# Attention probabilities turned by a VectorE block transpose and transfers inside SBUF, in place of identity products on TensorE

## The chip, the core and the metric

The kernel runs on one core of a Trainium2 chip. The metric is the device time of one execution in microseconds (us). The engines are named as the profile names them: PE is the matrix engine (PEld its weight loads), DVE the vector engine, ACT the scalar engine, POOL the GpSimd engine, and SP the engine whose queue issues nearly all DMA transfers here. SBUF is the on-chip memory of 128 partitions, PSUM the accumulators that PE writes.

## The reference, cut to what matters

Two layers over 256 tokens of width 1024, all in float32. Each layer has a token mixer and a gated MLP with a residual sum each:

```python
xn = rmsnorm(h) * norm1
u, q, k, v, g_pool, g_attn = split(xn @ w_in)        # widths 1024, 1536, 1536, 1536, 1024, 1024
pooled = centred_mean(u, windows 2/4/8/16) - u ;  pool_out = (pooled @ w_pool) * pool_scale
for g, (window, dilation) in enumerate(((128, 1), (512, 4), (2048, 16))):   # 4 heads of 128 each
    logits = q_g @ k_g.T * 128**-0.5 + rel_bias[bucket(j - i)][:, heads of g]    # keys out of reach: -1e30
    o_g, lse_g = softmax(logits) @ v_g, logsumexp(logits)
attn = sum_g softmax_over_groups(lse)_g * o_g
merged = sigmoid(g_pool) * (pool_out @ w_a) + sigmoid(g_attn) * (attn @ w_b)
h = h + merged @ w_o
h = h + (gelu(conv3(rmsnorm(h) @ w_up_a)) * (rmsnorm(h) @ w_up_g)) @ w_down
```

The three groups share one normalisation: the weighting by the groups' softmax denominators equals one softmax over all the keys of the three groups together. The kernel uses that.

## The kernel before, in words

**Precision by parts.** A product of two float32 matrices is made from fp32r parts: each operand is split into a high part (an ACT cast) and a low part (a DVE subtraction of the cast from the original), and high x high, low x high and high x low are summed in PSUM. Every weight goes through this split on the chip: class `Weights` loads 1 MB pieces on SP's queue into three buffers `raw` (line 117), casts them on ACT (line 177, `wh`) and subtracts on DVE (line 178, `wl`). Five pairs of `wh`/`wl` exist, and the split runs three pieces ahead of the product that uses it. The dilated groups 1 and 2 of attention stay in plain f32.

**Tokens.** Tokens are stored by parity: row m of tile t holds token 2m + t. So the 256 tokens are two tiles of 128 rows; the 256 keys of group 0, and for groups 1 and 2 the 128 keys of the same parity, make 512 columns of scores for each head and tile.

**One layer.** Values are made first, then the eight columns of the pooling branch (`proj`, lines 482 and 484 for its two runs of products), then queries and keys in six rounds of `PAIRS` with four projections each. From round 3 on attention is interleaved: after some of the projections one step is taken from a list, `steps`; the rest of the list is used up during the eight projections by `w_a`. For the heads of a layer the steps are

- `scores(hh)`: for each tile t, products of queries and keys into one PSUM tile `s_ps` (lines 870 and 875), DVE adds the bias from the table `bt` (881) and finds the row maximum (886), ACT takes the exponential and the row sum (889), DVE divides by the sum (891, 892);
- `turn(hh)`: the probabilities have queries on the partitions, and the product with the values needs keys there. Per tile four 128x128 blocks are turned by products with an identity matrix (904) into PSUM `pt_ps`; ACT and DVE copy them out as a high part `pth` (905) and low part `ptl` (910) for group 0, and in f32 as `pt` for groups 1 and 2 (907, 909);
- `weigh(hh)`: products of values and turned probabilities into `o_ps` (921, 925), split into `at2`.

The list takes the heads in pairs (a, b): scores a, turn a, scores b, weigh a, turn b, weigh b.

**The bias table.** `load_bias` loads the bias rows `rel_bias` (32 buckets by 12 heads) and a one-hot table of 33 rows by 5 kinds of 256 offsets. `build_bias` makes one product per kind from 33 rows with the high and one with the low part of the bias (line 374, `f_ps`), interleaved with the first projections of the pooling branch in layer 0. The result goes through DRAM (`fd`, then `sk` with 128 copies), and five loads with a skewed row pitch fetch it as `bt`.

**What sets the order.** The code is written as one stream. A scheduler turns it into one fixed order for each engine and for SP's queue, and inserts the semaphore waits; buffers of one tag are reused in turn (`bufs` says how many). An engine works off its order strictly, so whatever waits holds up what stands behind it. DMA completions are counted on eight semaphores used in turn, so a DMA also waits for the one issued eight before it.

Of the kernel before, what the change touches and what calls it, by code (L numbers as in the profile page):

```python
# [10 lines left out]
F32 = mybir.dt.float32  # L11
F32R = mybir.dt.float32r
# [4 lines left out]
P = 128  # L17
# [5 lines left out]
HPG = 4  # L23
NG = 3
NH = HPG * NG
# [8 lines left out]
NT = 5  # L34
# [5 lines left out]
ENTRY = 4  # L40
# [164 lines left out]
def encoder(ctx, tc, x, w_in, w_pool, pool_scale, w_a, w_b, w_o, norm1, norm2, w_up, conv_w,  # L205
            conv_b, w_down, rel_bias, norm_f, onehot, edges, out):
    nc = tc.nc
    const = ctx.enter_context(tc.tile_pool(name="const", bufs=1))
    wpool = ctx.enter_context(tc.tile_pool(name="weights", bufs=1))
    big = ctx.enter_context(tc.tile_pool(name="big", bufs=1))  # L210
    sm = ctx.enter_context(tc.tile_pool(name="small", bufs=2))
    acc = ctx.enter_context(tc.tile_pool(name="acc", bufs=4, space=bass.MemoryType.PSUM))
# [139 lines left out]
    bt = const.tile([P, HPG, NT * P], F32, name="bt")  # L352

    def load_bias():
        oh = big.tile([33, NT * 256], F32, tag="ybig", name="onehot_sb")
        nc.sync.dma_start(out=oh, in_=onehot)
        rb = sm.tile([33, NH], F32, tag="rb", bufs=1, name="rb")
        nc.vector.memset(rb, 1.0)
        nc.sync.dma_start(out=rb[0:32, :], in_=rel_bias)
        rh = sm.tile([33, NH], F32R, tag="ms", name="rh")  # L360
        rl = sm.tile([33, NH], F32R, tag="ms", name="rl")
        nc.vector.tensor_copy(rh, rb)
        nc.vector.tensor_sub(out=rl, in0=rb, in1=rh.bitcast(F32))
        ohr = big.tile([33, NT * 256], F32R, tag="m2", name="onehot_r")
        nc.scalar.copy(out=ohr, in_=oh)
        return rh, rl, ohr

    def build_bias(rh, rl, ohr):

        fsb = big.tile([HPG, NT * 256], F32, tag="q1", name="fsb")  # L370
        for n, g in enumerate((0, 0, 0, 1, 2)):
            ps = acc.tile([P, 512], F32, tag="acc", name="f_ps")
            for j, r in enumerate((rh, rl)):
                nc.tensor.matmul(
                    ps[:HPG, :256], r[:, g * HPG : (g + 1) * HPG], ohr[:, n * 256 : (n + 1) * 256],
                    start=(j == 0), stop=(j == 1),
                )
            nc.vector.tensor_copy(fsb[:, n * 256 : (n + 1) * 256], ps[:HPG, :256])
            yield

        n = HPG * NT * 256
        fd = dram.tile([1, n], F32, name="fd")
        nc.sync.dma_start(out=fd[0].rearrange("(h e) -> h e", h=HPG), in_=fsb)
# [190 lines left out]
    def v_sum(ps, x2, t, n, piece):  # L574
# [3 lines left out]
        for m, (part, w, j) in enumerate(passes):  # L578
# [2 lines left out]
                stop=(n == 3 and m == 5),  # L581
            )

    def two_parts(tag, name):


        return big.tile([P, KD, 2, 2, P], F32R, tag=tag, name=name)

    def begin_values_of_x():
# [24 lines left out]

        def square(t, n):
            cc = HALVES[n]
            junk = sm.tile([P, 512], F32, tag="p", bufs=3, name="junk")
            if n == 0:
                nc.scalar.activation(
                    junk, h[:, t, cc], AF.Square, scale=D**-0.5, accum_out=ss[t][:, n : n + 1]  # L620
                )
            else:
                nc.vector.scalar_tensor_tensor(
                    out=junk, in0=h[:, t, cc], scalar=1.0 / D, in1=h[:, t, cc],
                    op0=ALU.mult, op1=ALU.mult, accum_out=ss[t][:, n : n + 1],
                )
            if n == 0:
                nc.gpsimd.tensor_scalar_add(ss[t][:, 3:4], ss[t][:, 0:1], EPS)
            else:
                nc.gpsimd.tensor_add(out=ss[t][:, 3:4], in0=ss[t][:, 3:4], in1=ss[t][:, 1:2])  # L630
                return nc.gpsimd.tensor_tensor(out=rs[t], in0=ss[t][:, 3:4], in1=mhalf, op=ALU.pow)
# [117 lines left out]
    for l in range(DEPTH):  # L749
# [43 lines left out]
        g2 = gain(norm2[l])  # L793


        plh = big.tile([P, KD, 2, P], F32R, tag="ybig", name="plh")
# [67 lines left out]
        probs, ptiles = {}, {}  # L864

        def scores(hh):
            for t in range(2):
                ps = acc.tile([P, 512], F32, tag="acc", name="s_ps")
                for m, (a, b) in enumerate(((qh, kh), (qh, kl), (ql, kh))):
                    nc.tensor.matmul(  # L870
                        ps[:, 0:256], a[:, hh, t, :], b[:, hh].rearrange("p t m -> p (t m)"),
                        start=(m == 0), stop=(m == 2),
                    )
# [6 lines left out]
                s = sm.tile([P, 512], F32, tag="s", name="s")  # L880
                nc.vector.tensor_add(
                    out=s.rearrange("p (a b) -> p a b", a=2), in0=ps.rearrange("p (a b) -> p a b", a=2),
                    in1=bias_of(t, hh),
                )
                nm = sm.tile([P, 1], F32, tag="nm", name="nm")
                nc.vector.tensor_reduce(out=nm, in_=s, axis=AX.X, op=ALU.max, negate=True)
                z = sm.tile([P, 1], F32, tag="z", name="z")
                p = sm.tile([P, 512], F32, tag="p", bufs=3, name="p")
                nc.scalar.activation(p, s, AF.Exp, bias=nm[:, 0:1], accum_out=z)
                rz = sm.tile([P, 1], F32, tag="rz", name="rz")  # L890
                nc.vector.reciprocal(rz, z)
                nc.vector.tensor_scalar(
                    out=p, in0=p, scalar1=rz[:, 0:1], scalar2=0.5, op0=ALU.mult, op1=ALU.mult
                )
                probs[hh, t] = p

        def turn(hh):
            pth = sm.tile([P, 2, 2, P], F32R, tag="pth", bufs=1, name="pth")
            ptl = sm.tile([P, 2, 2, P], F32R, tag="us", name="ptl")
            pt = sm.tile([P, 2, 2, P], F32, tag="pt", bufs=1, name="pt")  # L900
            for t in range(2):
                ps = acc.tile([P, 4, P], F32, tag="acc", name="pt_ps")
                for b in range(4):
                    nc.tensor.transpose(ps[:, b, :], probs[hh, t][:, b * P : (b + 1) * P], ident)  # L904
                nc.scalar.copy(out=pth[:, :, t, :], in_=ps[:, 0:2, :])
                if t == 0:
                    nc.scalar.copy(out=pt[:, :, t, :], in_=ps[:, 2:4, :])
                else:
                    nc.vector.tensor_copy(pt[:, :, t, :], ps[:, 2:4, :])
                nc.vector.tensor_sub(  # L910
                    out=ptl[:, :, t, :], in0=ps[:, 0:2, :], in1=pth[:, :, t, :].bitcast(F32)
                )
            ptiles[hh] = pth, ptl, pt

        def weigh(hh):
            pth, ptl, pt = ptiles[hh]
# [14 lines left out]
            nc.vector.tensor_sub(out=ol, in0=ps, in1=oh.bitcast(F32))  # L931

        steps = []
        for pair in ((0, 1), (2, 3)):
            a, b = pair
            steps += [(scores, a), (turn, a), (scores, b), (weigh, a), (turn, b), (weigh, b)]

        def step():
            if steps:
                f, hh = steps.pop(0)  # L940
                f(hh)


        for m, c in enumerate(PAIRS):
# [7 lines left out]
            for n in range(4):  # L952
# [16 lines left out]
                else:  # L969
# [2 lines left out]
                    nc.vector.scalar_tensor_tensor(  # L972
                        out=o, in0=src, scalar=scale, in1=o, op0=ALU.mult, op1=ALU.add
                    )
                if m >= 3 and n % 2:
                    step()

        pa = big.tile([P, KD, S], F32, tag="ybig", name="pa")
        for c in range(KD):
            add_up(pa[:, c, :], proj(po2))  # L980
            if c not in (1, 6):
                step()
        assert not steps


        gates = big.tile([P, 4, S], F32, tag="gates", name="gates")
# [61 lines left out]

        a_first = big.tile([P, ENTRY, S], F32, tag="gates", name="a_first")

        def keep_entry(ps):
            r = sm.tile([P, ENTRY * P], F32, tag="p", bufs=3, name="a_rows")
            nc.scalar.copy(out=r, in_=ps)
            return r

# [5 lines left out]
            nc.vector.tensor_copy(av, pt)  # L1061

        held, ps = entry
        first = keep_entry(ps)
        ps = v_tile()
        for n in range(4):
            v_sum(ps, x2, 1, n, held[n])
# [1 line left out]
                turn_entry(0, first)  # L1069
        for i, _ in held:  # L1070
            W.free(i)
        last = keep_entry(ps)
        g_first = [proj(x2)]
        turn_entry(1, last)

# [96 lines left out]
```

## Time and profile before

| | |
|---|---|
| median of 3 runs | 882.49 us (881.98 to 882.96) |
| profiled execution, span | 880.5 us |
| PE busy | 872.5 us, 99% |
| DVE busy | 676.9 us, 77% |
| ACT busy | 520.3 us, 59% |
| DMA, all queues | 164.46 MB, 187 GB/s on the mean |

The profiled execution is one execution; its own time is given as its span from the first to the last instruction, and the medians of the runs include what lies around that span. A profile row gives start, duration, engine, source line, operation, and what is written and read. A matmul's duration includes the time in the pipeline, so that neighbours overlap: the time which a product takes from the engine is the distance from its start to the start of the next. "Granted clock" (PEclk) is the share of the full clock that PE was given. A transfer's "landing" is the time from its issue to its arrival.

### The profile page before, as it was taken

What the parts mean: (1) busy time and instruction counts of PE and PEld (TensorE: products, weight loads), DVE (VectorE), ACT (ScalarE), POOL (GpSimd) and SP (SyncE); (2) the same over time, 40 slices, a digit from 0 to 9 for tenths busy, and PEclk for the clock granted to TensorE, in tenths of its full rate; (3) what the DMA queues carried; (4) which work ended last, traced back from release to release, by engine and by line L of the source; (5) the groups of instructions that cost most, each with busy time, mean ns of one, the idle gap of its engine ahead of it and who ended that gap; (6) DMA issues with size and microseconds to landing.
All of it is one profiled execution on the core that took longest, in us unless ns stands there. A gap on an engine that the chain in (4) does not pass through costs nothing.

```text
span 880.5 us, 12819 instructions
## 1 busy us (share of the span) xinstructions
PE 872.5 (99%) x4849; PEld 759.1 (86%) x4849; DVE 676.9 (77%) x1151; ACT 520.3 (59%) x913; POOL 13.8 (2%) x40
## 2 busy tenths in 40 slices
PE   9999999999999999999999999999999999999996
PEld 7889889988888888888888898999888888888885
DVE  6987786767869987787756977776678698878774
ACT  7745654556648766666545564554566486666652
POOL 2000000000000000000000000000000000000000
PEclk9999999999999999999999999999999999999999
DMA  9669744455564665465736565443556447466541
GB/s 329 232 206 296 254 145 147 141 182 176 176 206 148 206 223 191 159 220 196 239 120 223 160 198 185 148 163 123 190 190 202 163 144 260 165 198 203 173 144 48
DMA packets 125789, 164.46 MB, mean 187 GB/s; under 512 B 2995, under 2 KB 106107, under 8 KB 125600
## 3 DMA queue, kind: packets, MB, share of 16 engines
q1 hardware_dynamic: 125712, 163.65, 56.0%
q8 instruction: 38, 0.62, 0.3%
q14 instruction: 23, 0.19, 0.1%
q10 hardware_dynamic: 16, 0.00, 0.0%
HBM read 162.57 MB, written 3.69 MB: 189 GB/s over the span
## 4 chain that ended last, share of the span: by engine, by line
PE 99%; ACT 0%; POOL 0%; DVE 0%; issue 0%; POOLq 0%; ACTq 0%
PE proj_ps L482 40%; PE proj_ps L484 21%; PE res_ps L510 6%; PE res_ps L509 6%; PE v_ps L579 6%; PE res_ps L511 6%; PE v_ps L741 2%; PE b_ps L482 2%; PE v_ps L654 1%; PE b_ps L484 1%; PE s_ps L875 1%; PE o_ps L925 1%; PE pt_ps L904 1%; PE s_ps L870 1%; PE o_ps L921 1%; PE xt_ps L450 1%
## 5 line engine op out<-in xcount | busy, mean ns | idle before, releaser
L178 DVE TENSOR_TENSOR wl<-raw,wh 128x1024 fp32r<-128x1024 f32 x274 | 334.1, 1222 | 137.8 <-ACT wh L177 135.4
L177 ACT CAST wh<-raw 128x1024 fp32r<-128x1024 f32 x274 | 286.1, 1049 | 194.7 <-PE proj_ps L482 134.4
L482 PE MATMUL proj_ps<-x,wh 128*128 128x512 f32 x1408 | 354.1, 393 | 0.0
L482 PEld LDWEIGHTS proj_ps<-x,wh 128*128 128x128 f32 x1408 | 254.1, 189 | 47.4 <-issue 0.5
L484 PEld LDWEIGHTS proj_ps<-x,wl 128*128 128x128 f32 x1408 | 192.0, 190 | 13.8
L484 PE MATMUL proj_ps<-x,wl 128*128 128x256 f32 x1408 | 196.3, 282 | 0.0
L509 PE MATMUL res_ps<-wh,actq 128*128 128x512 f32 (+1 forms) x184 | 70.2, 381 | 0.0
L510 PE MATMUL res_ps<-wl,actq 128*128 128x512 f32 (+1 forms) x184 | 70.1, 381 | 0.0
L511 PE MATMUL res_ps<-wh,actk 128*128 128x512 f32 (+1 forms) x184 | 69.9, 380 | 0.0
L511 PEld LDWEIGHTS res_ps<-wh,actk 128*128 128x128 f32 x184 | 34.6, 188 | 6.7
L509 PEld LDWEIGHTS res_ps<-wh,actq 128*128 128x128 f32 x184 | 34.7, 188 | 6.2
L510 PEld LDWEIGHTS res_ps<-wl,actq 128*128 128x128 f32 x184 | 34.7, 188 | 6.0
L482 PE MATMUL proj_ps<-po,wh 128*128 128x512 f32 x128 | 33.1, 400 | 0.0
L1102 ACT ACTIVATE y<-y 128x256 f32<-128x256 f32 x44 | 18.3, 416 | 24.6 <-DVE y L1099 24.6
L1085 ACT ACTIVATE y<-a,prm 128x256 f32<-128x256 f32 x36 | 21.6, 600 | 15.9 <-DVE a L505 15.9
L416 ACT ACTIVATE junk<-h 128x512 f32<-128x512 f32 (+1 forms) x20 | 10.9, 547 | 27.8 <-DVE h L414 27.8
L509 PE MATMUL res_ps<-wh,m 128*128 128x512 f32 (+1 forms) x72 | 26.5, 368 | 0.0
L482 PEld LDWEIGHTS proj_ps<-po,wh 128*128 128x128 f32 x128 | 22.9, 189 | 4.1
L510 PE MATMUL res_ps<-wl,m 128*128 128x512 f32 (+1 forms) x72 | 26.3, 366 | 0.0
L511 PE MATMUL res_ps<-wh,m 128*128 128x512 f32 (+1 forms) x72 | 26.3, 365 | 0.0
L579 PE MATMUL v_ps<-wh,x 128*128 128x512 f32 x80 | 25.7, 392 | 0.0
L1086 DVE SCALAR_TENSOR_TENSOR y<-a,prm,y 128x255 f32<-128x255 f32 x36 | 17.2, 479 | 8.1 <-ACT y L1085 8.1
(208 smaller groups left out, 1106.3 us busy)
## 6 DMA issues: line engine op xcount, KB each, us to landing
raw<-in_w_in_dram SPq DMA_DIRECT2D x58, 1024.0 KB, 5.1
raw<-in_w_up_dram SPq DMA_DIRECT2D x44, 1024.0 KB, 4.9
raw<-in_w_down_dram SPq DMA_DIRECT2D x22, 1024.0 KB, 4.8
raw<-in_w_a_dram SPq DMA_DIRECT2D x8, 1024.0 KB, 4.9
raw<-in_w_o_dram SPq DMA_DIRECT2D x8, 1024.0 KB, 4.8
raw<-in_w_b_dram SPq DMA_DIRECT2D x4, 1024.0 KB
sk<-fd SPq DMA_DIRECT2D x1, 2560.0 KB
raw<-in_w_pool_dram SPq DMA_DIRECT2D x2, 1024.0 KB
```

The costliest lines, as they stand in the source:

```text
L177: lambda: nc.scalar.copy(out=h, in_=src),
L178: lambda: nc.vector.tensor_sub(out=l, in0=src, in1=h.bitcast(F32)),
L482: nc.tensor.matmul(ps, wh(k), x2[:, k], start=(k == 0), stop=False)
L484: nc.tensor.matmul(ps[:, 1], wl(k), x2[:, k, 0], start=False, stop=(k == nk - 1))
L509: nc.tensor.matmul(ps, ah, wh, start=first, stop=False)
L510: nc.tensor.matmul(ps, ah, wl, start=False, stop=False)
L511: nc.tensor.matmul(ps, al, wh, start=False, stop=last)
L579: nc.tensor.matmul(ps, x2[:, 2 * n + j, part, t, :], w[:, j, :], start=(n + m == 0), stop=(n == 3 and m == 5),)
L741: nc.tensor.matmul(ps[t], a[:, k, t, :], w[:, j, :], start=(k + m == 0), stop=(k == KD - 1 and m == 2),)
L1085: nc.scalar.activation(y, a, AF.Identity, bias=b, scale=w1)
L1086: nc.vector.scalar_tensor_tensor(out=y[:, 1:], in0=a[:, : S - 1], scalar=w0, in1=y[:, 1:], op0=ALU.mult, op1=ALU.add)
L1102: nc.scalar.activation(y2, y2, AF.Tanh, scale=c)
```

## The change

1. `turn` has no products. The two tiles of a head are kept in one buffer `probs[hh]` of 128 x 1024, the exponential and the division work in place, and one DVE instruction transposes all its 32x32 blocks into `rows`. What is left is to exchange the partition blocks: `cross` issues 16 transfers on SP's queue, each from 32 partitions of `rows` to 32 partitions of `pt`, 1 KB per partition (32 KB each). A new step `parts` makes `pth` (ACT) and `ptl` (DVE) from `pt` in SBUF, and groups 1 and 2 read `pt` directly.
2. The list of steps is: scores a, scores b, turn a, parts a, weigh a, turn b, parts b, weigh b for each pair, started at the same round (rounds 3 on, three projections of four) and finished in the eight projections by `w_a`.
3. The bias: high part and low part stand in one operand of 128 rows (rows 0 to 32 and 64 to 96), each group's four heads at columns 0, 32 and 64. Two loads of the one-hot table and six of the bias fill it, POOL clears both buffers first, and three products of 512, 512 and 256 columns take the place of ten. The store to `fd` is three transfers instead of one.
4. Buffers: `rows` shares the buffer of the norm gains, so the load of `norm2` (`g2`) moves from the start of the layer to behind attention; `junk`, `rb` and `probs` share the tag "s"; `pth` shares the tag "us"; the two tiles of `keep_entry` (MLP entry) move to the large buffer "m2".

```diff
     def load_bias():
-        oh = big.tile([33, NT * 256], F32, tag="ybig", name="onehot_sb")
-        nc.sync.dma_start(out=oh, in_=onehot)
-        rb = sm.tile([33, NH], F32, tag="rb", bufs=1, name="rb")
-        nc.vector.memset(rb, 1.0)
-        nc.sync.dma_start(out=rb[0:32, :], in_=rel_bias)
...
+        oh = big.tile([P, NT * 256], F32, tag="ybig", name="onehot_sb")
+        nc.gpsimd.memset(oh, 0.0)
+        rb = sm.tile([P, P], F32, tag="s", name="rb")
+        nc.gpsimd.memset(rb, 0.0)
+        for r in (0, 64):
+            nc.sync.dma_start(out=oh[r : r + 33, :], in_=onehot)
+            for g in range(NG):
+                cc = slice(32 * g, 32 * g + HPG)
+                nc.sync.dma_start(out=rb[r : r + 32, cc], in_=rel_bias[:, g * HPG : (g + 1) * HPG])
...
     def build_bias(rr, ohr):
...
+        for c0, groups in ((0, (0, 0)), (512, (0, 1)), (1024, (2,))):
+            width = 256 * len(groups)
             ps = acc.tile([P, 512], F32, tag="acc", name="f_ps")
...
+            nc.tensor.matmul(ps[:, :width], rr, ohr[:, c0 : c0 + width], start=True, stop=True)
...
+    def cross(out, in_):
+
+        for i in range(4):
+            for j in range(4):
+                a, b = slice(32 * i, 32 * i + 32), slice(32 * j, 32 * j + 32)
+                nc.sync.dma_start(out=out[b, i], in_=in_[a, j])
...
         def turn(hh):
...
+            rows = sm.tile([P, 4, 2, 4, 32], F32, tag="gain", bufs=1, name="rows")
+            nc.vector.transpose(
+                out=rows.rearrange("p j t c r -> p (t c) j r"),
+                in_=probs[hh].rearrange("p t (c j r) -> p (t c) j r", c=4, j=4),
+            )
+            pt = sm.tile([P, 4, 2, 4, 32], F32, tag="pt", bufs=1, name="pt")
+            cross(pt, rows)
+            ptiles[hh] = pt
+
+        def parts(hh):
+            pt = ptiles[hh].rearrange("p i t c r -> p c t i r")
+            pth = sm.tile([P, 2, 2, P], F32R, tag="us", name="pth")
             ptl = sm.tile([P, 2, 2, P], F32R, tag="us", name="ptl")
-            pt = sm.tile([P, 2, 2, P], F32, tag="pt", bufs=1, name="pt")
-            for t in range(2):
-                ps = acc.tile([P, 4, P], F32, tag="acc", name="pt_ps")
-                for b in range(4):
-                    nc.tensor.transpose(ps[:, b, :], probs[hh, t][:, b * P : (b + 1) * P], ident)
...
+            for c in range(2):
+                hi, lo = (a[:, c].rearrange("p t (i r) -> p t i r", i=4) for a in (pth, ptl))
+                nc.scalar.copy(out=hi, in_=pt[:, c])
+                nc.vector.tensor_sub(out=lo, in0=pt[:, c], in1=hi.bitcast(F32))
+            ptiles[hh] = pth, ptl, pt[:, 2:4]
...
-        for pair in ((0, 1), (2, 3)):
-            a, b = pair
-            steps += [(scores, a), (turn, a), (scores, b), (weigh, a), (turn, b), (weigh, b)]
+        for a, b in ((0, 1), (2, 3)):
+            steps += [(scores, a), (scores, b), (turn, a), (parts, a), (weigh, a)]
+            steps += [(turn, b), (parts, b), (weigh, b)]
...
-                if m >= 3 and n % 2:
+                if m >= 3 and n and len(steps) > 8:
                     step()
```

More of the change, by code (lines that the diff above doesn't have):

```diff
@@ new lines, in load_bias @@
+        nc.gpsimd.memset(oh, 0.0)
[6 more added lines that the diff above has]
+                nc.sync.dma_start(out=rb[r : r + 32, cc], in_=rel_bias[:, g * HPG : (g + 1) * HPG])
+        for g in range(NG):
+            nc.gpsimd.memset(rb[32:33, 32 * g : 32 * g + HPG], 1.0)
@@ new lines, in load_bias, with build_bias @@
+        rr = big.tile([P, P], F32R, tag="at2", name="rr")
+        nc.vector.tensor_copy(rr, rb)
+        nc.vector.tensor_sub(
+            out=rr[64:96], in0=rb[64:96], in1=rr[64:96].bitcast(F32)
+        )
+        ohr = big.tile([P, NT * 256], F32R, tag="m2", name="onehot_r")
+        nc.scalar.copy(out=ohr, in_=oh)
+        return rr, ohr
+    def build_bias(rr, ohr):
+        fsb = big.tile([96, NT * 256], F32, tag="q1", name="fsb")
+        for c0, groups in ((0, (0, 0)), (512, (0, 1)), (1024, (2,))):
+            width = 256 * len(groups)
+            ps = acc.tile([P, 512], F32, tag="acc", name="f_ps")
+            nc.tensor.matmul(ps[:, :width], rr, ohr[:, c0 : c0 + width], start=True, stop=True)
+            for j, g in enumerate(groups):
+                cc = slice(j * 256, (j + 1) * 256)
+                rows = slice(32 * g, 32 * g + HPG)
+                nc.vector.tensor_copy(fsb[rows, c0 + j * 256 : c0 + (j + 1) * 256], ps[rows, cc])
@@ L382, in build_bias @@
         fd = dram.tile([1, n], F32, name="fd")
-        nc.sync.dma_start(out=fd[0].rearrange("(h e) -> h e", h=HPG), in_=fsb)
+        fv = fd[0].rearrange("(h e) -> h e", h=HPG)
+        for g, cc in enumerate((slice(0, 768), slice(768, 1024), slice(1024, 1280))):
+            nc.sync.dma_start(out=fv[:, cc], in_=fsb[32 * g : 32 * g + HPG, cc])
         sk = dram.tile([P, n + 1], F32, name="sk")
@@ L933, in encoder @@
         steps = []
-        for pair in ((0, 1), (2, 3)):
-            a, b = pair
-            steps += [(scores, a), (turn, a), (scores, b), (weigh, a), (turn, b), (weigh, b)]
+        for a, b in ((0, 1), (2, 3)):
+            steps += [(scores, a), (scores, b), (turn, a), (parts, a), (weigh, a)]
+            steps += [(turn, b), (parts, b), (weigh, b)]
         def step():
             if steps:
-                f, hh = steps.pop(0)
-                f(hh)
+                f, *which = steps.pop(0)
+                f(*which)
         for m, c in enumerate(PAIRS):
@@ L980, in encoder @@
             add_up(pa[:, c, :], proj(po2))
-            if c not in (1, 6):
-                step()
+            step()
         assert not steps
+        g2 = gain(norm2[l])
         gates = big.tile([P, 4, S], F32, tag="gates", name="gates")
@@ L1063, in encoder @@
         held, ps = entry
-        first = keep_entry(ps)
+        first = keep_entry(0, ps)
         ps = v_tile()
@@ L1071, in encoder @@
             W.free(i)
-        last = keep_entry(ps)
+        last = keep_entry(1, ps)
         g_first = [proj(x2)]
```

40 lines of the change are left out of this document (8 added, 32 removed).

## The prediction

> **What bounds the kernel.** I read the busy lines and the chain first, then PE's waits, then the stages around attention.
>
> ```profile
> PE 872.5 (99%) x4849; PEld 759.1 (86%) x4849; DVE 676.9 (77%) x1151; ACT 520.3 (59%) x913; POOL 13.8 (2%) x40
> ...
> PE 99%; ACT 0%; POOL 0%; DVE 0%; issue 0%; POOLq 0%; ACTq 0%
> ```
> ```profile
> PE gain_ps L333 <- DVE ones L319: 1.0, 1, 1.0
> PE v_ps L654 <- ACT xuh L610: 0.2, 1, 0.2
> ```
> ```profile
> 110.00:180.00 70.00, 70.00 (x452) 63.42 (x451) 51.34 (x92) 35.95 (x70) 0.00 (x0) 1.00 0.46 150
> 560.00:612.00 52.00, 52.00 (x337) 47.09 (x336) 35.85 (x64) 26.95 (x53) 0.00 (x0) 1.00 0.45 146
> ```
>
> The chain is PE alone, and PE waited for others 1.2 us in the whole run. The windows are the attention stages of the two layers (PE, PEld, DVE, ACT, POOL busy, clock, DMA share, GB/s): PE is full at clock 1.00, DVE is busy 73% and 69%, ACT 51% and 52%, the DMA engines under half. So an instruction taken off PE shortens the run by its start-to-start pace, unless what replaces it arrives late at PE.
>
> **Part 1: 64 transposes leave PE.** Eight per head, four heads, two layers.
>
> ```profile
> L904 PE MATMUL pt_ps<-ident,p x64: 271/272/273, 119.2 to 603.0; 128*128 128x128 f32 x64
> ```
> ```profile
> 112.04 0.28 PE L870 MATMUL s_ps<-kh,qh 128*128 128x256 f32 x1
> ...
> 113.57 2.09 PE L482 MATMUL proj_ps<-x,wh 128*128 128x512 f32 x8
> ...
> 116.45 2.00 PE L482 MATMUL proj_ps<-x,wh 128*128 128x512 f32 x8
> 118.29 1.11 PE L484 MATMUL proj_ps<-x,wl 128*128 128x256 f32 x8
> 119.24 1.03 PE L904 MATMUL pt_ps<-ident,p 128*128 128x128 f32 x8
> 120.03 2.10 PE L482 MATMUL proj_ps<-x,wh 128*128 128x512 f32 x8
> ...
> 122.92 2.00 PE L482 MATMUL proj_ps<-x,wh 128*128 128x512 f32 x8
> ```
>
> The 272 ns overlap; the pace is what counts. From the start of the transposes to that of the next projection are 120.03 - 119.24 = 0.79 us, and the projection behind them takes 122.92 - 120.03 = 2.89 instead of 116.45 to 119.24 = 2.79: another 0.10, the turn from f32 back to fp32r. So 0.89 a head, 8 x 0.89 = 7.1 us off the path.
>
> **Part 2: the bias table.** Five pairs of 33-row products become three 128-row products (512, 512, 256 columns).
>
> ```profile
> 42.16 1.84 PE L482 MATMUL proj_ps<-x,wh 128*128 128x512 f32 x7
> ...
> 45.95 2.11 PE L482 MATMUL proj_ps<-x,wh 128*128 128x512 f32 x8
> ...
> 55.89 2.11 PE L482 MATMUL proj_ps<-x,wh 128*128 128x512 f32 x8
> ...
> 58.79 2.00 PE L482 MATMUL proj_ps<-x,wh 128*128 128x512 f32 x8
> 60.63 1.12 PE L484 MATMUL proj_ps<-x,wl 128*128 128x256 f32 x8
> 61.59 1.78 PE L482 MATMUL proj_ps<-x,wh 128*128 128x512 f32 x7
> ```
>
> One projection alone takes 61.59 - 58.79 = 2.80. The five with a pair each take 58.79 - 42.16 = 16.63, so the pairs cost 16.63 - 5 x 2.80 = 2.63 us. A 512-column product paces (60.63 - 58.79)/8 = 0.23, a 256-column one (61.59 - 60.63)/8 = 0.12, so the three cost 0.58: 2.05 us saved. But they now stand in one place, inside the third projection, behind six small loads of the bias that wait for a POOL memset of a buffer which PE reads until about 42.4. Laid out with the rows below for an issue (0.33), a cast and a split, the operand is ready at about 49.9, and PE reaches it at 42.16 + 2 x 2.80 + 1.84 + 3 x 0.12 = 49.96. A tie: I charge 0.3 us, with 0 and 3 (two landings of the weights' kind too late) as bounds. The onehot memset and its second load are early and off the path; the one-hot cast on ACT keeps its 1280 columns; the copies out of PSUM stay five.
>
> **Part 3: what replaces the transposes.** Per head: one VectorE block transpose (128x1024), 16 transfers of 32 KB on SP's queue, two ACT casts and two DVE subtractions. Taken away: two casts, one ACT and one DVE copy, two subtractions.
>
> ```profile
> L905 ACT CAST pth<-pt_ps x16: 373/382/393, 119.9 to 603.5; 128x256 fp32r<-128x256 f32 x16
> L910 DVE TENSOR_TENSOR ptl<-pt_ps,pth x16: 410/414/415, 121.7 to 604.8; 128x256 fp32r<-128x256 f32 x16
> L907 ACT COPY pt<-pt_ps x8: 377/378/379, 120.1 to 603.2; 128x256 f32<-128x256 f32 x8
> L909 DVE COPY pt<-pt_ps x8: 410/413/415, 122.0 to 604.4; 128x256 f32<-128x256 f32 x8
> ```
> ```profile
> 117.27 1.22 DVE L178 TENSOR_TENSOR wl<-raw,wh 128x1024 fp32r<-128x1024 f32 x1
> ...
> 118.41 0.16 DVE L891 RECIPROCAL rz<-z 128x1 f32<-128x1 f32 x1
> ...
> 118.81 0.48 DVE L892 TENSOR_SCALAR p<-p,rz 128x512 f32<-128x512 f32 x1
> ...
> 127.56 1.28 DVE L881 TENSOR_TENSOR s<-s_ps,bt 128x512 f32<-128x512 f32 x2
> ...
> 128.76 1.27 DVE L886 TENSOR_REDUCE nm<-s 128x1 f32<-128x512 f32 x2
> ```
>
> No row shows a block transpose. Bounds: 0.98 (twice the 128x512 scaling, 0.49) and 2.4 (twice the 128x1024 subtraction); I take 1.22, the same shape. DVE gains 1.22 - 0.41 = 0.8 us a head, ACT loses 0.38; both lie in the 27 to 49% that these engines have free. What can reach PE is latency.
>
> ```profile
> 12.41 0.29 SPq L345 DMA_DIRECT2D prow<-in_conv_b_dram  x1
> 12.74 0.29 SPq L346 DMA_DIRECT2D prow<-in_pool_scale_dram  x1
> ```
> ```profile
> raw<-in_w_a_dram SPq DMA_DIRECT2D x8, 1024.0 KB, 4.9
> ...
> bt<-sk SPq DMA_DIRECT2D x5, 256.0 KB, 5.5
> ...
> out_dram<-xn SPq DMA_DIRECT2D x4, 256.0 KB, 2.3
> ```
> ```profile
> SPq L117 <- DVE wl L178: 197.7, 41, 9.0
> ```
>
> Small DMAs are issued 12.74 - 12.41 = 0.33 us apart. DMA completions are counted on eight semaphores in turn, so the ninth of the 16 waits until the first has landed. With a landing L, the last lands at the later of 5.0 + L and 2L + 2.3 after the first issue. L is bounded by 2.3 (256 KB out of SBUF, nothing else moving) and 5.5 (256 KB of short runs); I take 2.3, the nearest in kind: from SBUF, long runs, and the ring mostly empty by then. So 7.3 us.
>
> Now the first head of a pair, a, from the end of the second head's scores (time 0, which is 113.57 + 2.88 + 1.53 = 117.98 on the old clock: a projection, 116.45 - 113.57, and a score block, 113.57 - 112.04). In the new order DVE does, from 117.27 on, a split 1.22, two reciprocals 0.16, three query or key parts of 0.42, a scaling 0.48, the bias pair 1.28, the maxima 1.27, then the transpose 1.22: done at 6.3. The transfers have landed at 13.6, the first cast 0.38 later. PE meets the first product of a's weighing after five projections, eight products and four: 0.1 + 14.0 + 1.84 + 0.48 = 16.4. Slack 2.4 us. By the same steps: b's transfers share the buffer pt and wait on SP until PE has finished weighing a (18.5), land at 25.8, wanted at 30.5: 4.3 with the cast taken off; c 2.7; d 5.0. Casts and subtractions come out up to 0.1 behind PE at a weighing; eight waits ahead of the f32 products are further semaphore instructions. I charge 0.05 a head, 0.4 in all (bounds 0 and 3).
>
> **Queues behind the waits.** Behind the 16 transfers on SP stand the next weight loads. SP spent its time before waiting for buffers (the last row above is the largest of its waits), since three buffers of two pieces run ahead of DVE's splits; a load is wanted some four projections, 11.2 us, after its buffer is free, and then waits up to three more in split form. Landing 4.9 plus 5.3 of transfers and up to 2.3 of semaphore is 12.5, inside that. On ACT and DVE, casts of later weights stand behind the cast that waits for the landing; PE has about four split pieces, 11 us, in hand. The norm2 gain load (512 KB) now comes after attention, where the row buffer is free; it is used only behind w_o. I cost these three at nothing. If a landing comes 5 us late, that cover is gone as well.
>
> **Sum.** 7.1 + 2.05 - 0.3 - 0.4 = 8.45 off the profiled execution's 880.5 span. The median of the runs, 882.49, is 2 us above that span and carries the same difference: 882.5 - 8.4 = 874.1.
>
> **Rivals.**
> First, the other side: the transfers land like the short-run load, L = 5.5. Then the last is in after 2 x 5.5 + 2.3 = 13.3, 6.0 later than I count, and PE stands 3.6 + 3.3 + 1.7 + 1.0 = 9.6 us a layer at the weighings, 19.2 in all: 893. It eats the whole gain from L = 4.8 on (4x - 14.4 = 4.2, x = 4.65). For it: 1 KB runs on one queue with the weights, two rounds of eight. Against it: the 2.3 row, and that the loads just ahead are issued several us earlier.
> The Trainium skill speaks for this one: DMA: Bandwidth & Descriptors, Rules for kernel authors, wants many small transfers made into one, those under 64 KB being mostly overhead; here each is 32 KB. The out_dram row bounds that overhead at 2.3 us, and two rounds of it fit the slack; no row shows it for transfers inside SBUF. Another rule would deepen it: TensorE: Matmul & The Clock Gate, Part 1, halves PE's clock after an idle window of about 3.4 us; the stops of 3.6 would then add, as an estimate, up to 1.7 each, 3 us in all. No gap in this trace is long enough to show that.
>
> Second, partial waits: transpose at 2.4 and L = 3.6 to 4.2. The first rows are 1.2 later and the landing 2.2 to 3.4 later; a and c then wait 0.7 to 2.2 each, b not or little: 2 to 7 us in all, 876 to 881.
>
> Third, starved weights: DVE's second transpose waits until the first row buffer has been read, and the splits behind it on DVE wait too. From a stop of about 11 us PE runs dry; a projection or two a pair lost, 2.8 each, four pairs: 880 to 890. DVE's free quarter speaks against it.
>
> Fourth, the change takes nothing off the path: some late chain just fills the room. PE's lack of waits speaks against it: 881 to 884.
>
> **How the numbers follow.** Forecast 0.58; first rival 0.17; second 0.13; third 0.07; fourth 0.05. The forecast's own range is 872.8 (nothing charged, a few tenths better) to 876. With the second rival, the fourth and the lower part of the third, 872.5 to 886 holds about 0.8. Beyond 0.2% (1.8 us, about what can be told here): faster 0.58 + 0.13 + 0.03 = 0.74; same 0.04 from the fourth; slower 0.17 + 0.05 = 0.22.
>
> **What would show it.** Right: no pt_ps on PE; 2.80 between projections without a jump; three f_ps products within 0.6 us; PE waits of under 1 us at the weighings; transfers on SP about 0.33 apart, 7 us from first issue to last landing; a block transpose near 1.2 us. Wrong: PE waiting at o_ps for the ACT cast or a DMA, PE's share below 98%, a clock below 1.00 in 110 to 180, issues that stop after the eighth transfer, or PE waiting for wh.

## The result, and the profile after

The changed kernel takes 886.86 us (median of four runs, 885.75 to 887.9) beside 882.48 us before: ratio 1.0054, 95% interval 1.0042 to 1.0065. It is 4.4 us slower, where 8.4 us were to be gained. Two of its four runs took about 886 us and two about 888, and what sets them apart is not shown; the profile is of one of the former. The profiled execution spans 884.3 us, with a granted clock of 1.00 in both attention stages.

From the page of the changed kernel, the busy line and the two lines of the chain:

```profile
PE 868.0 (98%) x4778; PEld 752.8 (85%) x4778; DVE 682.5 (77%) x1150; ACT 518.7 (59%) x905; POOL 14.7 (2%) x45
...
PE 82%; SPq 8%; DMA 3%; DVE 3%; issue 1%; ACT 1%; ACTq 0%; POOLq 0%; POOL 0%; DVEq 0%
PE proj_ps L491 30%; PE proj_ps L493 16%; SPq L598 8%; PE res_ps L518 6%; PE v_ps L588 6%; PE res_ps L519 6%; PE res_ps L520 6%; PE v_ps L757 2%; PE b_ps L491 2%; DMA pt<-rows 2%; PE v_ps L670 1%; DMA raw<-in_w_in_dram 1%; PE o_ps L939 1%; PE o_ps L943 1%; PE b_ps L493 1%
```

PE has 71 products fewer and is busy 4.5 us less, but it idles more: 884.3 - 868.0 = 16.3 us against 880.5 - 872.5 = 8.0. The chain, which was 99% PE, now runs for 8% of the span through SP's issues at line 598, the sixteen transfers. The longest waits of PE, and who waited for the transfers:

```profile
PE o_ps L939 <- ACT pth L929: 8.3, 7, 1.9
```
```profile
L598 SPq DMA_DIRECT2D pt<-rows x128: 512/589/1630, 122.8 to 620.6; - x128
...
  DMA pt<-rows: 16.0, 8
```

Seven of the eight weighings make PE stand, 8.3 us in all. ACT's cast `pth`, which PE waits for, has itself waited eight times (16.0 us) for the last transfer. One head of layer 0, by the timelines of DVE, SP, ACT and PE:

```profile
121.54 1.23 DVE L915 STREAM_TRANSPOSE rows<-probs 128x1024 f32<-128x1024 f32 x1
```
```profile
122.79 10.91 SPq L598 DMA_DIRECT2D pt<-rows  x16
133.80 1.14 SPq L117 DMA_DIRECT2D raw<-in_w_a_dram  x2
```
```profile
135.01 0.71 ACT L929 CAST pth<-pt 128x256 fp32r<-128x256 f32 x2 [3.32 <-DMA pt<-rows]
```
```profile
117.06 2.09 PE L491 MATMUL proj_ps<-x,wh 128*128 128x512 f32 x8
...
132.95 0.63 PE L493 MATMUL proj_ps<-x,wl 128*128 128x256 f32 x4
135.47 0.38 PE L939 MATMUL o_ps<-pth,vh 128*128 128x256 f32 x1 [1.89 <-ACT pth L929]
135.69 0.64 PE L493 MATMUL proj_ps<-x,wl 128*128 128x256 f32 x4
```

The block transpose ends at 122.77. SP then issues for 10.91 us, 0.68 us a transfer. The last transfer is there 1.3 us after the last issue has ended (135.01 against 122.79 + 10.91 = 133.70), so it is the issuing that takes the time and not the landing. PE comes to the first product of the weighing at 132.95 + 0.63 and stands 1.89 us, in the middle of a projection.

The stage of attention, from the first `s_ps` to the first `b_ps` of a layer, gives the account:

```profile
111.12 0.28 PE L886 MATMUL s_ps<-kh,qh 128*128 128x256 f32 x1
...
213.41 1.09 PE L491 MATMUL b_ps<-at,wh 128*128 128x512 f32 x4
...
544.79 0.28 PE L886 MATMUL s_ps<-kh,qh 128*128 128x256 f32 x1
...
648.02 1.09 PE L491 MATMUL b_ps<-at,wh 128*128 128x512 f32 x4
```

Before, the stage of layer 0 runs from 112.04 (the first `s_ps`) to this row, that of layer 1 from 543.67 to 643.89:

```profile
212.27 1.09 PE L482 MATMUL b_ps<-at,wh 128*128 128x512 f32 x4
```

| | layer 0, us | layer 1, us |
|---|---|---|
| before | 100.23 | 100.22 |
| before, less 4 x 0.89 for the transposes | 96.67 | 96.66 |
| changed kernel | 102.29 | 103.23 |
| of it PE's waits at `o_ps` | 3.66 | 4.63 |

Against the row without transposes the layers lose 5.6 and 6.6 us, 12.2 in all. Of that 8.3 are the waits. Of the remaining 3.9, 0.7 stay when nothing waits (e6, below). The other 3.2 lie around the seven stops, 0.4 to 0.5 each. Two pieces of that can be read at the stop above. The marked wait begins where the last product before it ends, at 132.95 + 0.63 = 133.58, but at the pace of 0.12 the next could have started at 133.43. And from the first product to the next it is 0.22 us (135.47 to 135.69), where the same product takes 0.12 among its own kind (136.09 to 136.21 in e6). That is 0.25 together; where the rest goes is not shown. Outside attention the stages differ by under 1 us.

### The profile page after: what moved, and what is told of

Its sections match the earlier page's. It is cut to its first block, busy times and chain, and to the rows that moved or that the text cites. A ratio compares the mean times of both kernels' runs of the same rounds, so it can differ in the third digit from the quotient of the medians.

```text
span 884.3 us, 12920 instructions
## 1 busy us (share of the span) xinstructions
PE 868.0 (98%) x4778; PEld 752.8 (85%) x4778; DVE 682.5 (77%) x1150; ACT 518.7 (59%) x905; POOL 14.7 (2%) x45
## 4 chain that ended last, share of the span: by engine, by line
PE 82%; SPq 8%; DMA 3%; DVE 3%; issue 1%; ACT 1%; ACTq 0%; POOLq 0%; POOL 0%; DVEq 0%
PE proj_ps L491 30%; PE proj_ps L493 16%; SPq L598 8%; PE res_ps L518 6%; PE v_ps L588 6%; PE res_ps L519 6%; PE res_ps L520 6%; PE v_ps L757 2%; PE b_ps L491 2%; DMA pt<-rows 2%; PE v_ps L670 1%; DMA raw<-in_w_in_dram 1%; PE o_ps L939 1%; PE o_ps L943 1%; PE b_ps L493 1%
## 5 line engine op out<-in xcount | busy, mean ns | idle before, releaser
L425 ACT ACTIVATE junk<-h 128x512 f32<-128x512 f32 (+1 forms) x20 | 10.9, 547 | 27.7 <-DVE h L423 27.7
```

## The experiments

There is one theory at the start: SP's own time for an issue makes the probabilities late, and PE, which works in a fixed order, stands. It has two rivals: the transfers themselves are slow, or the new order costs on PE whatever arrives when. "Before" in these comparisons took 881.85 to 882.05 us.

### One part at a time

`e1_bias_only` is the kernel before with the new `load_bias` and `build_bias`; `e2_turn_only` is the changed kernel with the old ones.

```diff
 # e1, against the kernel before; e2 has these lines the other way round, against the changed kernel
-        for n, g in enumerate((0, 0, 0, 1, 2)):
+        for c0, groups in ((0, (0, 0)), (512, (0, 1)), (1024, (2,))):
...
-                    ps[:HPG, :256], r[:, g * HPG : (g + 1) * HPG], ohr[:, n * 256 : (n + 1) * 256],
+            nc.tensor.matmul(ps[:, :width], rr, ohr[:, c0 : c0 + width], start=True, stop=True)
```

> The kernel before with the new bias table alone; the probabilities are turned by products as before. If the table works as the prediction's part 2 has it (ten short products replaced by three, 2.05 us saved, 0.3 charged), 882.5 - 1.75 = 880.7. If it gives what the trace of the changed kernel shows at the first pool product (1.41 us ahead), 881.1. If the late loads of the bias rows cost as much as the products save, 882.5 or more.

> The changed kernel with the old bias table: the new way of turning alone. If the loss lies at the weighings of the probabilities and the table saves 1.4 us, 886.9 + 1.4 = 888.3, with the same waits of PE at o_ps (8 us in all). If the table is what costs, 885 or less.

Measured: the table alone 880.72 us, ratio 0.9985 (0.9976 to 0.9995); the turning alone 888.6 us, ratio 1.0068 (1.0053 to 1.0083). The table gains 1.2 us and the new way of turning loses 6.7. That 880.72 meets the first expectation of e1 is partly luck: it reckoned with 882.5 for the kernel before, which took 881.94 here, and the gain of 1.2 is nearer the 1.4 of the second. For e2 the first expectation came out, with waits at `o_ps` of 8.8 us. Together that makes 5.5 us lost, not the 4.4 of the change; of it e2's profiled execution lost 1.7 to a halved clock (last section). In e1, PE's rows around the three products:

```profile
42.54 2.07 PE L491 MATMUL proj_ps<-x,wh 128*128 128x512 f32 x8
...
50.58 0.85 PE L381 MATMUL f_ps<-onehot_r,rr 128*128 128x512 f32 x3
51.27 0.76 PE L493 MATMUL proj_ps<-x,wl 128*128 128x256 f32 x5
...
57.48 2.00 PE L491 MATMUL proj_ps<-x,wh 128*128 128x512 f32 x8
```

Five projections with the three products take 57.48 - 42.54 = 14.94 us, where they took 16.63 with the five pairs: 1.69 less. The products themselves take 0.69, and PE doesn't wait.

### Issues on a second queue: ACT, POOL

```diff
-                nc.sync.dma_start(out=out[b, i], in_=in_[a, j])
+                (nc.scalar if j % 2 else nc.sync).dma_start(out=out[b, i], in_=in_[a, j])    # e3
+                (nc.gpsimd if j % 2 else nc.sync).dma_start(out=out[b, i], in_=in_[a, j])    # e7
```

> The changed kernel; of the 16 transfers of a head eight are issued on SP's queue and eight on ACT's. Theory: SP needs 0.63 to 0.69 us for each issue, so 16 take 10 to 11 us, and this alone makes the probabilities late. Then each queue is done in about 5.3 us, PE's waits at o_ps (8.3 us) go nearly to nothing, and the time is 875 to 878, or up to 2 us more where ACT, busy with issuing for 5 us a head, is late with a cast. Rival, the transfers themselves are slow (landing, or sharing the DMA engines with the weights): the waits stay and the time is 886 to 888. Rival, the new order on PE costs whatever arrives when: 884 or more, with few waits at o_ps.

> The changed kernel; of the 16 transfers of a head eight are issued on SP's queue and eight on POOL's, an engine that is 2% busy, so nothing waits behind the issues as it did on ACT. If SP's issue time is what made the probabilities late and POOL issues as fast, the last landing comes 4 to 5 us earlier and PE's waits at o_ps fall from 8.3 us to under 3: 875 to 880. If POOL needs longer for an issue than SP (over 1 us each), eight of them take 8 to 10 us, little is won and the time is 882 to 887. The planner may also put the products earlier, since it knows of two queues; then waits of a us or so stay.

Measured: with ACT 885.79 us, 1.0037 (1.0024 to 1.005); with POOL 884.15 us, 1.0025 (1.0014 to 1.0036). Both gain little over the changed kernel, and the forecasts of 875 to 880 failed; only the last sentence for e7, on earlier places, came true. The transfers did come earlier. In e7 the timelines of SP, POOL, ACT and PE for the first head show:

```profile
122.07 5.01 SPq L598 DMA_DIRECT2D pt<-rows  x8
```
```profile
122.35 4.15 POOL L598 DMA_DIRECT2D pt<-rows  x8 [79.98 <-DVE rows L915]
```
```profile
129.00 0.71 ACT L929 CAST pth<-pt 128x256 fp32r<-128x256 f32 x2 [0.81 <-DMA pt<-rows]
```
```profile
127.60 1.33 PE L491 MATMUL proj_ps<-x,wh 128*128 128x512 f32 x5
129.46 0.39 PE L939 MATMUL o_ps<-pth,vh 128*128 128x256 f32 x1 [0.53 <-ACT pth L929]
```

The cast starts 6.9 us after the first issue instead of 12.2. But in this kernel's order PE comes to the products at 127.60 + 1.33 = 128.9, 12.6 us behind the second head's scores instead of 16.5, and stands again: the scheduler has placed them earlier. Why it did is not shown; in e5, below, where the data come earlier too, it placed them later. Across the run PE still waits 4.3 us for these products (2.9 for `pth`, 1.4 in smaller waits), and the two attention stages, 102.17 and 99.71 us, are 8 us above what they can be; what the unmarked part of that is, these runs don't settle. On ACT the issues also hold up ACT's own work, 38 us in all. Its longest group of waits in e3:

```profile
ACT q L989 <- DMA pt<-rows: 20.5, 4, 5.7
```

So the transfers themselves are fast once they are issued. What counts is the distance between the arrival and the place that PE's order has for the products, and each of these changes to the transfers moved both.

### Which transfers take 0.6 us to issue

```diff
+    src = bt.rearrange("p h e -> p (h e)")
...
+    lo, hi = slice(0, 32), slice(32, 64)
+    for k in range(4):
+        nc.sync.dma_start(out=dst[hi, 256 * k : 256 * k + 256], in_=src[lo, 256 * k : 256 * k + 256])
+    for k in range(4):
+        nc.sync.dma_start(out=dst[lo, 256 * k : 256 * k + 256], in_=src[lo, 256 * k : 256 * k + 256])
...
```

In this manner follow 256 B runs to partitions 64 to 95, 16 partitions, 32 and 96 partitions to a DRAM buffer `far`, 32 partitions back from it, all 128 partitions inside SBUF, and the first group again on ACT's queue.

> The kernel before with nine groups of four transfers added behind its last product; it computes the same, and its own time means nothing, only what an issue of each shape takes on its queue. If the 0.59 us belong to every transfer of 32 partitions inside SBUF: 0.59 for the first group (32 partitions x 1 KB to other partitions), for the second (the same partitions) and for the third (256 B runs), and 0.3 to 0.4 for 128 partitions. If they belong to crossing partitions, the second group takes 0.3. If they come from a queue that is crowded during attention, all groups take 0.3 to 0.4 here. If they go with the number of partitions, 16 take less than 32 and 128 take far more than 0.59. On ACT's queue (last group) the same as on SP's.

The groups by line, each with min, median and max of an issue in ns; the lines stand in the order of the diff:

```profile
L1148 SPq DMA_DIRECT2D dst<-bt x4: 507/579/582, 717.1 to 719.6; - x4
L1150 SPq DMA_DIRECT2D dst<-bt x4: 588/588/589, 720.2 to 722.1; - x4
L1152 SPq DMA_DIRECT2D dst<-bt x4: 507/588/590, 722.7 to 724.8; - x4
L1154 SPq DMA_DIRECT2D dst<-bt x4: 587/664/765, 728.0 to 730.1; - x4
L1156 SPq DMA_DIRECT2D far<-bt x4: 414/496/1294, 90.4 to 97.9; - x4
...
L1161 SPq DMA_DIRECT2D got<-far x4: 340/460/570, 699.2 to 703.7; - x4
L1163 SPq DMA_DIRECT2D got<-bt x4: 491/558/601, 704.4 to 707.5; - x4
L1165 ACTq DMA_DIRECT2D got<-bt x4: 600/602/607, 699.2 to 701.1; - x4
```

Of the expected splits only the start of the first came out. Inside SBUF an issue takes 0.56 to 0.66 us in the median with 16, 32 or 128 partitions, with 256 B or 1 KB runs, to the same partitions or to others, on SP or ACT, outside attention too. With DRAM at one end the probe's shapes take 0.46 to 0.50. Among these shapes the price goes with the transfer and not with its size: sixteen cost sixteen times.

### Five transfers over DRAM in place of sixteen

```diff
-        for i in range(4):
-            for j in range(4): ... nc.sync.dma_start(out=out[b, i], in_=in_[a, j])
+        turned = dram.tile([P, 4, 256], F32, name="turned")
+        nc.sync.dma_start(out=turned, in_=in_.rearrange("p j t c r -> p j (t c r)"))
+        for j in range(4):
+            src = turned[:, j].rearrange("(i q) x -> q i x", i=4)
+            nc.sync.dma_start(out=out[32 * j : 32 * j + 32].rearrange("p i t c r -> p i (t c r)"), in_=src)
```

> The changed kernel; the 16 transfers of a head are replaced by one store of the transposed blocks to DRAM (512 KB) and four loads of 128 KB that pick them up in the new order, all on SP's queue. Theory (issuing is what costs): one store, about 2.5 us until it is there, four issues of about 0.5 us and another 2.5 us: some 7 us instead of 12.2 from first issue to last landing, so PE's waits at o_ps nearly go, 875 to 878. Rival (landing is what costs): two landings one behind the other are as late as before or later, 887 or more. Rival (the order on PE costs): 884 or more with few waits.

Measured: 874.46 us, 0.9914 (0.9898 to 0.9931): 7.5 us faster than the kernel before, and half a microsecond below the range expected. PE waits at `o_ps` nowhere, and the attention stages take 97.19 and 97.20 us. SP's, ACT's and PE's rows for the first head:

```profile
122.22 0.34 SPq L596 DMA_DIRECT2D turned<-rows  x1
124.83 1.76 SPq L599 DMA_DIRECT2D pt<-turned  x4
```
```profile
133.86 0.70 ACT L930 CAST pth<-pt 128x256 fp32r<-128x256 f32 x2
```
```profile
116.50 2.09 PE L491 MATMUL proj_ps<-x,wh 128*128 128x512 f32 x8
...
134.51 0.29 PE L940 MATMUL o_ps<-pth,vh 128*128 128x256 f32 x1
```

The last issue ends 4.4 us after the start of the first, instead of 10.9. But the cast, which waits for no transfer here, stands as late as 133.86 in ACT's order, and PE's order has the first product 134.51 - 116.50 = 18.0 us after the second head's scores, where the changed kernel has it after 133.58 - 117.06 = 16.5. So this run changed the arrival and the place together; the next one separates them.

### The same sixteen transfers, the products later

The transfers stay as in the change. `weigh` is held back behind a projection that PE does later, and the steps have fixed places; the gates use another buffer, because the low part of the values has to live longer.

```diff
+        def weigh_behind(hh):
+            with tc.issue_after(newest[0].ins):      # the last product of the newest projection
+                weigh(hh)
+        places = {
+            (3, 1): [(scores, 0)], (3, 2): [(scores, 1)], (3, 3): [(turn, 0)],
+            (5, 1): [(parts, 0), (weigh_behind, 0), (turn, 1)],
+            ("a", 0): [(scores, 2)], ("a", 1): [(scores, 3)],
+            ("a", 2): [(parts, 1), (weigh_behind, 1), (turn, 2)],
+            ("g", 0): [(parts, 2), (weigh_behind, 2), (turn, 3)],
+            ("g", 5): [(parts, 3), (weigh_behind, 3)],
+        }                                            # "a": projections by w_a, "g": by the gates
...
-        gates = big.tile([P, 4, S], F32, tag="gates", name="gates")
+        gates = big.tile([P, 4, S], F32, tag="q1", name="gates")
```

> The changed kernel with all its 16 transfers a head on SP, but the products that need them stand later in PE's order: head a's behind the seventh projection after the scores instead of inside the sixth, b's two projections later than now, c's one later, d's two later; the buffer of the gates moves, since the low part of the values must be read longer. Theory: the only loss is that PE reaches these products before the probabilities do; the waits at o_ps (8.3 us, and about 3 more for stopping and starting inside a projection) go, and the time is 875 to 877. Rival, SP's 40 us of issuing also starve the weight loads, or the casts that wait for landings hold up the weights' casts: PE then waits at proj_ps, 878 or more. Rival, the transfers slow whatever runs beside them: 884 or more without waits of PE.

Measured: 873.98 us, 0.9909 (0.9894 to 0.9924), 1.0 below the range expected. SP still issues for 10.64 us at the first head, and PE waits for nothing in attention:

```profile
122.19 10.64 SPq L600 DMA_DIRECT2D pt<-rows  x16
```
```profile
116.45 2.09 PE L491 MATMUL proj_ps<-x,wh 128*128 128x512 f32 x8
...
135.14 1.11 PE L493 MATMUL proj_ps<-x,wl 128*128 128x256 f32 x8
136.09 0.28 PE L941 MATMUL o_ps<-pth,vh 128*128 128x256 f32 x1
136.21 0.28 PE L941 MATMUL o_ps<-ptl,vh 128*128 128x256 f32 x1
```

The stages take 97.07 us (110.52 to 207.59) and 96.98 us (538.97 to 635.95). That settles it: with the transfers unchanged, giving them more room (at the first head 136.09 - 116.45 = 19.6 behind the scores, against 16.5) brings the time to the forecast. The second pair's scores also stand earlier here, at 146.08 instead of 150.83, which adds to the room of its two heads. Slow transfers, starved weights and casts held up by the landings would all have shown here, and PE doesn't wait at `proj_ps`.

### Both cures, and places that are early

`e8_dram_later` is the one with the DRAM way and the later places; `e9_dram_early` has the DRAM way with the products pinned early: they stand behind one projection, and the next projection stands behind them.

```diff
 # e9, places:
+            (4, 3): [(parts, 0), (weigh_behind, 0), (turn, 1)],
+            ("a", 0): [(scores, 2)],
+            ("a", 1): [(parts, 1), (weigh_behind, 1), (scores, 3), (turn, 2)],
+            ("a", 6): [(parts, 2), (weigh_behind, 2), (turn, 3)],
+            ("g", 2): [(parts, 3), (weigh_behind, 3)],
 # and the projection that follows a weighing stands behind its last product:
+            with tc.issue_after(pin[0].ins): two_sums(...)
```

> Both cures at once: the way over DRAM (one store, four loads a head) and the later places of the products. Theory: each alone already leaves PE without a wait at o_ps, and what is left is the length of PE's own work, so the two together give the same as each, 873.8 to 874.6. Rival, SP's 80 us of issuing still cost something in the kernel with the later places (weight loads behind them): then 1 us or more is won, below 873.2.

> The way over DRAM with the products pinned to places that are as early as in the changed kernel or earlier: head a's behind the fifth projection after the scores (the changed kernel has them inside the sixth), b's behind the second projection by w_a, c's behind the seventh, d's behind the third of the gates; the gates' buffer moves as for the later places. Theory: what counts is when the data are there against when PE comes. PE comes to head a at 116.5 + 5 x 2.8 = 130.6; the store is issued at 122.2, landed 2.6 later, the last of the four loads is issued at 126.6, and with the 2.3 of an output store it has landed at 128.9, its cast done at 129.7: no wait, 873.8 to 875.5. Rival, places this early cost in themselves: 880 or more, as in the changed kernel. If a load out of DRAM takes the 5 us of a weight piece, PE waits about 2 us at each of the four, 886 or so.

Measured: e8 874.29 us, 0.9919 (0.9902 to 0.9935), with stages of 96.81 and 96.93 us: the same as each cure alone, as expected, so that nothing of SP's issuing is left on the path in e6. e9 895.97 us, 1.0149 (1.0126 to 1.0173): the slowest of all, though its data come early. The forecast of 873.8 to 875.5 failed, and the rival's 880 or more came. Six of the eight weighings now make PE stand twice, for `pth` and for `ptl`. The waits of PE, and ACT's order ahead of the first head's cast:

```profile
PE o_ps L946 <- ACT pth L936: 5.5, 6, 1.1
PE o_ps L946 <- DVE ptl L937: 5.4, 6, 1.0
```
```profile
130.63 1.05 ACT L177 CAST wh<-raw 128x1024 fp32r<-128x1024 f32 x1 [1.46 <-PE proj_ps L491]
...
131.85 0.70 ACT L936 CAST pth<-pt 128x256 fp32r<-128x256 f32 x2
```

The last load's issue ends at 127.4, and the cast waits for no transfer. It stands in ACT's order behind a weight's cast that itself waits for PE, so it begins at 131.85, while PE is there at about 131.5. My expectation counted the transfers and one cast, and left out the work queued ahead of that cast. Only this head was followed up.

## Why the prediction was wrong

The forecast had the mechanism right: PE stands where the probabilities come late. Its sum was right as a sum too. One duration under it was not, the time from one issue of SP to the next.

- **Part 1, the transposes: right.** 7.1 us less 0.4 at the weighings was charged. In e6 and e8 the two attention stages together are 6.4 and 6.7 us shorter than before.
- **Part 2, the bias table: right in place, a little high in size.** Its 1.75 was 1.69 in e1's five projections. The run of the table alone gains 1.2, since in its profile the start of the kernel is 0.4 later (the first `r_ps` at 20.43 instead of 20.05). The table needn't be the cause: e5 to e9 have the same one and start at 19.5 to 19.9. In the changed kernel another 0.4 goes at the first pooling product, which comes before DVE has its low part (0.24 of it a marked wait).
- **Block transpose: right.** Taken as 1.22, measured 1.24, and done at 122.77, 5.7 after the second head's scores where I had counted 6.3.
- **Landing: right.** Taken as 2.3. From the start of the last issue (133.70 - 0.59) to the cast it is 1.9 us. So the first rival's cause (L = 5.5) is wrong, and its conclusion nearly right: it had the last transfer in at 13.3 us after the first issue, where 12.2 were measured.
- **Issue pace: wrong; this is the step that failed.** I took 0.33 us from two small loads out of DRAM (the `prow` rows), so that the last of sixteen was issued at 5.0 and landed at 7.3. Measured is 0.59 an issue and 0.63 start to start. With it and the landing of 1.9 my own formula gives 15 x 0.63 + 1.9 = 11.4, and four of the eight heads took 11.3 to 11.6 us from the first issue to the cast. In the other four one issue took 1.0 to 1.6 us, and they took 11.8 to 12.6; what held that issue is not shown. The first head of layer 0 is one of these, with 12.2: 4.9 late.
- **Slacks: about right, and with the measured arrival they give the waits of a layer.** I had 2.4, 4.3, 2.7 and 5.0 us. Minus 4.9, and 0.6 back from the earlier transpose, that makes PE stand 1.9, 0, 1.6 and 0, 3.5 in all, where 3.66 and 4.63 were measured. Head by head it fits layer 0 (1.89, none, 1.36 and 0.41) and not layer 1 (1.31, 0.89, 1.19 and 1.24). There the long issues fall on the second and the fourth head, in layer 0 on the first and the fourth. The first head's place was right: I had PE there 16.4 us after the scores, measured is 16.5. The arrival was off.
- **Price of a stop: too low.** I counted only the standing. Around each there was another 0.4 to 0.5, in all 3.2 us.
- **Queues behind the waits, the gain load: right at nothing.** PE never waited for a weight.
- **The other rivals.** The second, partial waits of 876 to 881, had the form right (in layer 0 the first heads of the pairs wait, the others hardly; in layer 1 all four wait) and the size too small. The third, starved weights, and the fourth, nothing off the path, are refuted by e6, which is faster by the forecast's gain with the same transfers.
- **The bounds.** I bounded the landing from both sides, 2.3 and 5.5, but not the pace, although the trace of before holds five loads in a row whose issues took 0.59 to 1.34 us each. Even with their shortest the forecast's own formula gives 15 x 0.594 + 2.3 = 11.2 instead of 7.3, more than the first head's slack of 2.4 covers:

```profile
L390 SPq DMA_DIRECT2D bt<-sk x5: 594/808/1335, 72.6 to 76.2; - x5
```

The Trainium skill (DMA: Bandwidth & Descriptors, Rules for kernel authors) wants many small transfers made into one. I weighed that as a matter of landing. The runs bear the rule out for the time of issuing: in e5 five transfers replace sixteen and 4.4 us replace 10.9. For the kernel's time they don't need it: e6 keeps the sixteen and is as fast.

## What to carry to other kernels

When a matrix engine that never waits hands work to a queue of transfers, count the transfers times the issue time of that very kind, then the cast and what is queued ahead of it, and set the sum against the place of the consumer in the final order; here moving the eight weighings back, the first by 3.1 us, was worth 12.9 us against the changed kernel, 11.5 of it in the attention stages of the profiles. In these runs a consumer put just ahead of its data cost time, and one put a projection later than it need be cost nothing. A price taken from another kind of transfer is a guess, and needs bounds like any other.

## What the runs showed of the hardware

An issue of a transfer inside SBUF took 0.56 to 0.66 us in the median, from 8 to 128 KB, and on POOL 0.50 with 32 KB. An issue close behind others was longer than one alone: a 1 MB weight load alone took 0.37 (the kernel before), and the two right behind the sixteen 1.14 together (the row at 133.80). A 512 KB store to DRAM, issued alone in e5, took 0.34.

A short stop came right before a halved clock of PE. In e2 one stop was 2.16 us long instead of 1.89, and then the granted clock fell. The window 132 to 140 (PE, PEld, DVE, ACT, POOL busy, clock, DMA share, GB/s) and PE's rows:

```profile
132.00:140.00 8.00, 5.84 (x27) 5.01 (x26) 5.01 (x7) 2.87 (x6) 0.00 (x0) 0.80 0.51 166
```
```profile
136.87 0.58 PE L930 MATMUL o_ps<-pth,vh 128*128 128x256 f32 x1 [2.16 <-ACT pth L920]
...
139.38 0.41 PE L930 MATMUL o_ps<-ptl,vh 128*128 128x256 f32 x1
139.60 0.41 PE L930 MATMUL o_ps<-pth,vl 128*128 128x256 f32 x1
...
140.24 0.29 PE L930 MATMUL o_ps<-pth,vl 128*128 128x256 f32 x1
140.36 1.05 PE L934 MATMUL o_ps<-pt,v 128*128 128x128 f32 x8
```

Products of 256 columns start 0.21 us apart until 140.24 and 0.12 apart after it: about 3.4 us at half speed, (1 - 0.80) x 8 = 1.6 us lost behind a stop of 2.2. In e9, with two stops of about 1 us close together, the clock falls behind five of the six double stops. The first of these stretches, in the same columns:

```profile
173.90:177.20 3.30, 3.30 (x13) 2.91 (x12) 0.42 (x1) 0.37 (x1) 0.00 (x0) 0.50 1.05 362
```

Five stretches of 3.4 us at half speed lose 8.5 us, beside 10.9 us of waits; together they are most of e9's 21.7 us over e8. The Trainium skill (TensorE: Matmul & The Clock Gate, Part 1) puts the half clock after an idle window of about 3.4 us. Here the half-speed stretch had that length, and in e2 a stop of 2.2 us was enough to bring it on. In the profiled execution of the changed kernel no stop did, nor did the longest of e3, 2.0 us.
